# A two-layer attention and retention trunk on one core: column parts in the first T stages, merged row transposes and y stores, and five smaller moves

## The chip, the cores and the metric

The kernel runs on one core of a Trainium2 chip. A core has five engines, each with its own instruction stream: TensorE (PE, matrix products, with a separate record for loading weights, PEld), VectorE (DVE), ScalarE (ACT), GpSimd (POOL) and SyncE (SP), which issues the DMA transfers here. The metric is the device time of one execution in microseconds (us), as the median of several runs. TensorE's clock is regulated: the profile states the granted clock as a share of full speed.

## The reference

Two layers, 2048 tokens, width 1024. Each layer normalizes x, projects it to 4096 columns (eight parts of 512: queries, keys, values and gate of attention; the same of retention), runs two mixers and adds the product of their gated outputs with w_out.

```python
def hybrid_layer(x, norm_gain, w_in, w_out, rel_bias, cos, sin):
    hn = rms_norm(x, norm_gain)
    aq, ak, av, ag, rq, rk, rv, rg = jnp.split(hn @ w_in, cuts, axis=-1)
    ya = chunked_rel_attention(aq, ak, av, rel_bias)      # 8 heads of 64
    yr = chunkwise_retention(rq, rk, rv, cos, sin)        # 4 heads of 128
    y = jnp.concatenate([ya * silu(ag), yr * silu(rg)], axis=-1)
    return x + y @ w_out
```

Attention works on chunks of 64 tokens, each over its own chunk and the eight before, with a learned bias per clipped distance, and a softmax. Retention rotates q and k by position (the tables cos and sin), multiplies within a chunk by a decay, carries a 128x128 state per head from chunk to chunk, and normalizes each head's output by its root mean square. After two layers there is a last normalization. All inputs and outputs are f32.

## The kernel before

**Precision.** Products are made of halves in f16: a value is a high half and a low half (the rest), and a product is three matmuls (high x high, high x low, low x high). So nearly every tensor stands twice: hTh and hTl are the two halves of the normalized tokens, transposed (features on the partitions), whT and wlT those of the weights, rot the halves of the rotated q and k, pq those of the softmax's exponentials.

**Tiling.** The tokens are cut into four blocks n of 512 (tiles of 128: a = 0 to 3), and the heads into four groups s (two attention heads, hx = 0 and 1, and one retention head). For each layer l, group s and block n there is a T stage, `dense_T` (L609): four sections j = 0 to 3 (attention q, attention k, retention k and q), each of 24 matmuls of 512 columns (L731) into an accumulator of the pool psD, which has two buffers; `evacuate` copies each out of it and makes its halves, on ACT, DVE and by DMAs. Then there is a V stage, `dense_V` (L738): for each tile a of 128 tokens 24 matmuls (L752) give the values and the gates; ACT takes them out (v, gt, rv, L760 to L763), and DVE makes the rests and finishes the gate (L766 to L770). gt has a ring of five buffers. After four groups, `wout` makes the output projection (dO, L1105), adds x, and prepares the next layer's tokens; `wout_first` does the beginning of it for the first tokens already in the last group: it loads y from DRAM, squares and scales it, splits it in halves (rhy and rly) and has them transposed (L236, L237).

**Attention and retention of a block** run between the matmuls of the next block's stages, as a generator of 24 steps, one unit (a, hx) every three. For a unit, `qk` makes the logits S on TensorE (L800, L801); DVE adds the bias and takes the maximum in one instruction (L804), and multiplies it and adds a constant (L806); ACT takes the exponential (L807) and its high half (L809), POOL the rest (L810); a DMA on SP transposes both (pT, L812). Two units later `pv` multiplies with the values (L820 to L822), and `out_` divides by the sum, multiplies by the gate into ya, and stores it (L826, L827, L832, L835). `retention` does likewise for its head: products r (L860), state sh and its rest (L864, L868), the norm (a DVE instruction L920, a power on POOL L921), and yr, which is stored by itself (L925, L927).

**What sets the order.** The order is written out by hand: `run` takes steps from a dense stage and steps the attention beside it, and at each step (a tick) `later(k, ...)` work that is due is issued; `push` enters side work (weights, token rows, tables), of which `pull` takes pieces. In the first group the rows of tokens 4 to 15 are normalized, split and transposed while the stages already run. Each engine does its instructions in order; the order on SP is set by a scheduler. A tile's buffer is reused in turn by tag: "sc" and "pq" (two each) hold the logits and the halves of a unit, and at the layer end also the rows of y; "tabc", "tabs", "qq" and "swp" (one each) hold the rotary tables and what is swapped, and in wout the transposed y.

Of the kernel before, what the change touches and what calls it, by code (L numbers as in the profile page):

```python
# [18 lines left out]
P = 128  # L19
# [8 lines left out]
def hybrid_trunk(ctx: ExitStack, tc: tile.TileContext, x, pos, gain, gcol, w_in, w_out, rel, fgain,  # L28
# [33 lines left out]
    pool.memset(mhalf, -0.5)  # L62
    invf_sb = cp.tile([P, 1], F32, tag="invf", name="invf_sb")
# [6 lines left out]
    tab_d = [dp.tile([2, P, 512], F32, tag=f"tab{n}", name=f"tab{n}") for n in range(NS)]  # L70
# [12 lines left out]
    def tables(n, wk):  # L83

        ang, k, r, k2 = wk
# [40 lines left out]
        for hf in range(2):  # L126
            sl = slice(hf * 64, hf * 64 + 64)
            cs = slice(hf * 256, hf * 256 + 256)
            sp.dma_start(tab_d[n][0, 0:64, cs], k2[sl, :])
            sp.dma_start(tab_d[n][0, 64:128, cs], k2[sl, :])  # L130
            sp.dma_start(tab_d[n][1, 0:64, cs], ang[sl, :])
            sp.dma_start(tab_d[n][1, 64:128, cs], r[sl, :])
# [82 lines left out]
    def hT_of(l, n):  # L215
        if (l, n) not in hT:
            hT[l, n] = (hp.tile([P, KT, 512], F16, tag="hTh", name=f"hTh{l}_{n}"),
                        hp.tile([P, KT, 512], F16, tag="hTl", name=f"hTl{l}_{n}"))
        return hT[l, n]

    def row_pair(nm):
        return (b2.tile([P, 1280], F16, tag="sc", name=f"rh{nm}")[:, 0:D],
                b2.tile([P, 1280], F16, tag="pq", name=f"rl{nm}")[:, 0:D])
# [11 lines left out]
    def transpose_rows(rows, dh, dl):  # L235
        sp.dma_start_transpose(out=dh, in_=rows[0])  # L236
        sp.dma_start_transpose(out=dl, in_=rows[1])  # L237

    class Tok:


        def __init__(self, t, xt, rows):
            self.t, self.x, self.rows, self.nm = t, xt, rows, f"n0_{t}"
            self.hh, self.hl = (h_[:, :, t % 4 * P:(t % 4 + 1) * P] for h_ in hT_of(0, t // 4))
# [21 lines left out]
        def hi(self):  # L266
            if self.rows:
                self.rw = (self.rows[:, 0:D], self.rows[:, D:2 * D])
                act.activation(self.rw[0], self.x, AF.Copy)
                return  # L270
            for h in range(2):
                act.activation(self.hh[:, h * KT // 2:(h + 1) * KT // 2, :], self.pt[h], AF.Copy)

        def lo(self):
            if self.rows:
                dve.tensor_tensor(self.rw[1], self.x, self.rw[0], op=ALU.subtract)
                return
# [4 lines left out]
        def dma(self):  # L282
            transpose_rows(self.rw, self.hh, self.hl)
# [324 lines left out]
    def dense_T(l, s, n, g, st):  # L608
        hh, hl = hT[l, n]  # L609
        nm = f"{l}_{s}_{n}"  # L610
        st.tabc = b1.tile([P, 512], F32, tag="tabc", name=f"tabc{nm}")
        st.tabs = b1.tile([P, 512], F32, tag="tabs", name=f"tabs{nm}")
        def tab_load():
            while n not in tab_done:
                pull(1)
            sp.dma_start(st.tabc, tab_d[n][0])
            sp.dma_start(st.tabs, tab_d[n][1])
# [9 lines left out]
        def evacuate(j, ps):  # L627
            if j == 0:
                st.q = b2.tile([P, 2, 2, 512], F16, tag="q", name=f"q{nm}")
                qq = b1.tile([P, 2, 512], F16, tag="qq", name=f"qq{nm}")  # L630
# [10 lines left out]
            elif j == 1:  # L641
                st.k = b3.tile([P, 2, 512], F16, tag="k", name=f"k{nm}")
                kk = b1.tile([P, 2, 512], F16, tag="swp", name=f"kk{nm}")
                kh, kl = kk[:, 0, :], kk[:, 1, :]
                act.activation(kh, ps, AF.Copy, scale=2.0 ** -16)

                def k_rest():
                    dve.scalar_tensor_tensor(out=kl, in0=ps, scalar=2.0 ** -16, in1=kh, op0=ALU.mult, op1=ALU.subtract)
                    sp.dma_start(st.k[0:64, 0, :], kh[0:64, :])
                    sp.dma_start(st.k[64:128, 1, :], kh[64:128, :])  # L650
                    sp.dma_start(st.k[64:128, 0, :], kl[0:64, :])
                    sp.dma_start(st.k[0:64, 1, :], kl[64:128, :])

                soon(k_rest)
            else:
                w = 5 - j
                rot = b2.tile([P, w, 512], F16, tag=f"rot{j}", name=f"rot{nm}_{j}")
                if j == 2:
                    raw = rot[:, 1:3].rearrange("p a c -> p (a c)").bitcast(F32)
                else:  # L660
                    raw = b1.tile([P, 512], F32, tag="qq", name=f"raw{nm}")
                act.activation(raw, ps, AF.Copy, scale=2.0 ** -16)

                def swap(rot=rot, raw=raw, j=j):
                    swp = b1.tile([P, 512], F32, tag="swp", name=f"swp{nm}_{j}")
# [20 lines left out]
                    later(d, turned(raw, raw, st.tabc, ALU.mult))  # L686
                    later(d + 1, turned(swp, swp, st.tabs, ALU.mult))
# [30 lines left out]
        for j in range(2 if first else 0, 4):  # L718
# [19 lines left out]
    def dense_V(l, s, n, g, st):  # L738
        hh, hl = hT[l, n]
# [38 lines left out]
    def attention(l, s, n, g, st, prev, nxt):  # L778
# [4 lines left out]
        ya = {}  # L783

        def qk(a, hx):
# [10 lines left out]
            for j0, j1 in zip(cuts, cuts[1:]):  # L796
# [5 lines left out]
            v = b2.tile([P, 640], F32, tag="sc", name=f"sc{u.nm}")[:, 0:w]  # L802
            m = b2.tile([P, 1], F32, tag="mq", name=f"mq{u.nm}")
            dve.tensor_tensor_reduce(out=v, in0=S[:, 0:w], in1=g.bias[hx][:, 640 - w:640], scale=1.0, scalar=-3.0e38,  # L804
                                     op0=ALU.add, op1=ALU.max, accum_out=m)
            dve.tensor_scalar(m, m, g.nc[:, 0:1], LN_PSC, op0=ALU.mult, op1=ALU.add)  # L806
            act.activation(v, v, AF.Exp, bias=m[:, 0:1], scale=g.c[:, 0:1])  # L807
            pq = b2.tile([P, 1280], F16, tag="pq", name=f"pq{u.nm}")
# [6 lines left out]
        def pv(u):  # L815
            t = 4 * n + u.a
            o = psR.tile([P, 512], F32, tag="small", name=f"o{u.nm}")
            for b, (q_, a_) in enumerate(u.kts):
# [3 lines left out]
                pe.matmul(o[:, 0:65], u.p[:, u.nb + b, :], v_[:, 0:65], start=False, stop=(b == u.nb - 1))  # L822

            def out_():
                rl = b2.tile([P, 1], F32, tag="rl", name=f"rl{u.nm}")
                dve.reciprocal(rl, o[:, 64:65])  # L826
                dve.tensor_tensor(rl, rl, g.ka, op=ALU.mult)  # L827
                if u.hx == 0:
                    ya[u.a] = b2.tile([P, P], F32, tag="ya", name=f"ya{u.nm}")
                y = ya[u.a]  # L830
                vs = slice(u.hx * 64, u.hx * 64 + 64)
                dve.scalar_tensor_tensor(out=y[:, vs], in0=o[:, 0:64], scalar=rl[:, 0:1], in1=st.g[u.a][:, vs],  # L832
                                         op0=ALU.mult, op1=ALU.mult)
                if u.hx == 1:
                    sp.dma_start(y_d[t][:, s * P:(s + 1) * P], y)  # L835
# [3 lines left out]
        ret = retention(l, s, n, g, st)  # L839
# [30 lines left out]
    def decayed(l, s, n, g, st, a):  # L870
        nm = f"{l}_{s}_{4 * n + a}"
        cs = slice(a * P, (a + 1) * P)
        r1 = psR.tile([P, 512], F32, tag="small", name=f"r1{nm}")
        products(r1[:, 0:P], [(st.rk[:, i, cs], st.rq[:, j, cs]) for i, j in ((0, 0), (0, 1), (1, 0))])

        def upper():
            st.dT = b1.tile([P, 2, P], F16, tag="dT", name=f"dT{nm}")
            upper_of(st.dT, r1[:, P:2 * P])

        later(1, lambda: dve.tensor_tensor(r1[:, P:2 * P], r1[:, 0:P], g.msk, op=ALU.mult))  # L880
        later(2, upper)
        later(3, lambda: rest_of(st.dT, r1[:, P:2 * P]))

    def retention(l, s, n, g, st):
        for a in range(4):
# [12 lines left out]
            if not last:  # L898
# [16 lines left out]
                later(3, lambda sh=sh, ns=ns: rest_of(sh, ns))  # L915
# [7 lines left out]
            def fin(t=t, a=a, r2=r2, ss=ss, nm=nm):  # L923
                y = b1.tile([P, P], F32, tag="yr", name=f"yr{nm}")
                dve.scalar_tensor_tensor(out=y, in0=r2[:, 0:P], scalar=ss[:, 0:1], in1=st.g[a][:, P:256],  # L925
                                         op0=ALU.mult, op1=ALU.mult)
# [589 lines left out]
```

## Time and profile before

| | before |
|---|---|
| median of 3 runs | 2094.7 us (2092.41 to 2094.73) |
| the profiled execution | 2094.75 us |
| its span, first to last instruction | 2092.8 us |
| mean granted TensorE clock | 0.991 |
| PE busy | 2004.4 us, 14014 matmuls |
| DVE busy | 1343.8 us |
| ACT busy | 1141.3 us |
| POOL busy | 432.9 us |

In the profile's lines a group is: line of the kernel, engine, operation, what it writes <- what it reads with the shapes, how often; then busy time, mean nanoseconds of one, the idle time of the engine ahead of these instructions, and what ended it. In a timeline a line is start, duration, engine and line, operation; a bracket gives the idle time before it and what ended it. SPq lines are DMAs as SP issues them; their transfer lands later. PE's ends are modelled, so starts are the surer numbers.

### The profile page before, as it was taken

The page shows a single profiled execution, that of the slowest core. Times are in us where ns is not written, and L with a number is a line of the kernel's source. Part 1 is how long each engine was busy: PE and PEld are TensorE (multiplying, and loading weights), DVE is VectorE, ACT ScalarE, POOL GpSimd, SP SyncE. Part 2 cuts the span into 40 slices and gives each one's busy share as a digit, 9 for nine tenths or more (in the row PEclk, how much of TensorE's full clock was granted, in tenths as well). Part 3 has the DMA queues.
Part 4 walks back from the last instruction along what each step waited for, and adds up shares of the span by engine and source line. Part 5 has one row for each costly group of instructions (what it writes and reads, how often), then busy time and mean ns, then how long its engine had stood idle before and what let it go on. Part 6 is the DMA issues. An engine that isn't in the chain of part 4 may idle for free.

```text
span 2092.8 us, 39599 instructions
## 1 busy us (share of the span) xinstructions
PE 2004.4 (96%) x14014; PEld 1049.4 (50%) x14014; DVE 1343.8 (64%) x4031; ACT 1141.3 (55%) x2522; POOL 432.9 (21%) x509
## 2 busy tenths in 40 slices
PE   6888999999999999998999999999999999998998
PEld 4344455555555555444444555555555555554443
DVE  7676666666656666576654666666666667656643
ACT  7455665556565654455444546554655565455432
POOL 1022222222122212121000222222222222222100
PEclk9999999999999999999999999999999999999999
DMA  8767674557476764599965556655655776558874
GB/s 247 171 127 162 136 166 114 115 112 159 110 169 133 161 166 99 113 211 260 219 185 113 120 102 142 130 121 106 155 123 118 178 156 162 117 100 183 212 199 123
DMA packets 645702, 313.65 MB, mean 150 GB/s; under 512 B 459232, under 2 KB 602080, under 8 KB 645504
## 3 DMA queue, kind: packets, MB, share of 16 engines
q1 hardware_dynamic: 645504, 311.12, 66.4%
q8 instruction: 110, 1.80, 0.4%
q14 instruction: 88, 0.72, 0.1%
HBM read 123.26 MB, written 41.98 MB: 79 GB/s over the span
## 4 chain that ended last, share of the span: by engine, by line
PE 55%; DMA 7%; DVE 5%; ACT 3%; issue 1%; SPq 1%; POOL 0%; POOLq 0%; DVEq 0%; ACTq 0%
PE dT L731 18%; PE dV L752 15%; PE dO L1105 12%; DMA pT<-pq 2%; PE r L860 2%; PE S L801 2%; PE S L800 2%; PE o L820 1%; PE o L821 1%; PE o L822 1%; DVE sc L804 1%; DMA swp<-rot 1%; DMA yhy<-rhy 1%; ACT sc L807 1%; ACT pq L809 1%
## 5 line engine op out<-in xcount | busy, mean ns | idle before, releaser
L810 POOL TENSOR_TENSOR pq<-sc,pq 128x640 f16<-128x640 f32 (+4 forms) x256 | 323.8, 1265 | 1175.9 <-issue 590.7
L807 ACT ACTIVATE sc<-sc,mq,cT 128x640 f32<-128x640 f32 (+4 forms) x256 | 218.5, 853 | 558.1 <-DVE mq L806 413.7
L752 PE MATMUL dV<-whV,hTh 128*128 128x512 f16 x1024 | 354.5, 382 | 13.0 <-DVE gt L770 12.8
L731 PE MATMUL dT<-hTh,whT 128*128 128x512 f16 x1008 | 349.4, 382 | 14.7 <-DMA hTh<-hTl 9.6
L752 PE MATMUL dV<-wlV,hTh 128*128 128x512 f16 x1024 | 354.1, 381 | 0.0
L752 PE MATMUL dV<-whV,hTl 128*128 128x512 f16 x1024 | 354.0, 381 | 0.0
L731 PE MATMUL dT<-hTl,whT 128*128 128x512 f16 x1008 | 346.6, 379 | 0.0
L731 PE MATMUL dT<-hTh,wlT 128*128 128x512 f16 x1008 | 346.6, 379 | 0.0
L752 PEld LDWEIGHTS <-hTh 128*128 128x128 f16 x2048 | 197.3, 98 | 227.7 <-DVE gt L770 16.4
L731 PEld LDWEIGHTS <-whT 128*128 128x128 f16 x2016 | 192.9, 98 | 221.6 <-issue 24.1
L804 DVE CUSTOM_DVE_ANT_0 sc<-S,bias 128x640 f32<-128x640 f32 (+4 forms) x256 | 188.4, 736 | 78.8 <-PE S L801 61.1
L1105 PE MATMUL dO<-whO,yly 128*128 128x512 f16 x512 | 194.1, 379 | 2.4 <-DMA yly<-rly 2.4
L1105 PE MATMUL dO<-whO,yhy 128*128 128x512 f16 x512 | 194.0, 379 | 1.2 <-DVE gt L770 0.6
L1105 PE MATMUL dO<-wlO,yhy 128*128 128x512 f16 x512 | 194.0, 379 | 0.0
L809 ACT ACTIVATE pq<-sc 128x640 f16<-128x640 f32 (+4 forms) x256 | 171.5, 670 | 10.9 <-DMA pT<-pq 3.0
L1105 PEld LDWEIGHTS <-yhy 128*128 128x128 f16 x1024 | 99.6, 98 | 115.1 <-issue 0.8
L752 PEld LDWEIGHTS <-hTl 128*128 128x128 f16 x1024 | 99.7, 98 | 105.0 <-issue 2.8
L800 PE MATMUL S<-k,q 128*128 128x128 f16 (+3 forms) x592 | 143.1, 268 | 7.9 <-DVE mq L804 7.9
L731 PEld LDWEIGHTS <-wlT 128*128 128x128 f16 x1008 | 97.2, 98 | 101.8 <-issue 1.1
L820 PE MATMUL o<-v,pT 128*128 128x65 f16 x1120 | 129.6, 193 | 10.2 <-DMA pT<-pq 9.7
L801 PE MATMUL S<-k,q 128*128 128x128 f16 (+3 forms) x592 | 130.5, 268 | 0.0
L820 PEld LDWEIGHTS <-pT 128*128 128x128 f16 x1120 | 105.3, 97 | 49.2 <-DMA pT<-pq 21.3
(350 smaller groups left out, 3352.7 us busy)
## 6 DMA issues: line engine op xcount, KB each, us to landing
q<-qq SPq DMA_DIRECT2D x128, 128.0 KB, 2.7
yyy<-y_d SPq DMA_DIRECT2D x32, 512.0 KB, 4.6
stT<-in_w_in_dram SPq DMA_DIRECT2D x27, 512.0 KB, 4.8
stV<-in_w_in_dram SPq DMA_DIRECT2D x26, 512.0 KB, 4.5
k<-kk SPq DMA_DIRECT2D x128, 64.0 KB, 2.0
swp<-rot SPq DMA_DIRECT2D x64, 128.0 KB, 2.5
tabc<-tab SPq DMA_DIRECT2D x32, 256.0 KB, 2.7
tabs<-tab SPq DMA_DIRECT2D x32, 256.0 KB, 2.9
```

Of the source, the lines that this page charges most:

```text
L731: pe.matmul(ps, w_[:, j, kt, :], h_[:, kt, :], start=(m == 0), stop=(m == 23))
L752: pe.matmul(ps, h_[:, kt, a * P:(a + 1) * P], w_[:, kt, :], start=(m == 0), stop=(m == 23))
L800: pe.matmul(o, st.q[:, hx, 0, cs], k_, start=True, stop=False)
L801: pe.matmul(o, st.q[:, hx, 1, cs], k_, start=False, stop=True)
L804: dve.tensor_tensor_reduce(out=v, in0=S[:, 0:w], in1=g.bias[hx][:, 640 - w:640], scale=1.0, scalar=-3.0e38, op0=ALU.add, op1=ALU.max, accu ...
L807: act.activation(v, v, AF.Exp, bias=m[:, 0:1], scale=g.c[:, 0:1])
L809: act.activation(pq[:, 0:w], v, AF.Copy)
L810: pool.tensor_tensor(pq[:, w:2 * w], v, pq[:, 0:w], op=ALU.subtract)
L820: pe.matmul(o[:, 0:65], u.p[:, b, :], v_[:, 0:65], start=(b == 0), stop=False)
L821: pe.matmul(o[:, 0:64], u.p[:, b, :], v_[:, 65:129], start=False, stop=False)
L860: pe.matmul(out_, w_, m_, start=(i == 0), stop=(i + 1 == len(pairs)))
L1105: pe.matmul(ps, h_[:, kt, :], w_[:, kt, :], start=(m == 0), stop=(m == 23))
```

## The change

1. In the T stages of the first group's blocks n = 1, 2, 3, sections 0 and 1 are made in column parts: token tile by token tile, both sections in turn, 24 matmuls of 128 columns each, with both accumulators open at once.
2. A token's (or y's) high and low rows stand side by side in one tile and are turned by one DMA transpose instead of two; hTh and hTl are one tile, as are the transposed halves of y. The logits' tags "sc" and "pq" become one tile, the rotary tables one, which is loaded in one DMA, and the tables are stored in four DMAs instead of eight. qq, kk, raw and swp become tiles of one tag.
3. y is written into the gate's own tile gt, and attention's and retention's halves of a token tile are stored by one DMA, when both are finished.
4. The logits' scale goes into the reduction as its operand (the minimum of the negative logits in place of the maximum); the multiply and add L806 becomes an addition of a constant on POOL.
5. Both heads of a token tile share one accumulator tile; the reciprocal and its factor are taken for both at once.
6. The rest of retention's state is issued four ticks after, not three.
7. wout_first is pushed after prep_O(l, 1) and the weights' preparation, not ahead of it.

```diff
-        ang, k, r, k2 = wk
+        ang, r, k2, k = (wk[:, i * 256:(i + 1) * 256] for i in range(4))
...
-    def transpose_rows(rows, dh, dl):
-        sp.dma_start_transpose(out=dh, in_=rows[0])
-        sp.dma_start_transpose(out=dl, in_=rows[1])
+    def transpose_rows(rows, dst):
+        sp.dma_start_transpose(out=dst, in_=rows[2])
...
+        second = (l, s) == (0, 0) and n > 0
+        if second:
+            ps = [psD.tile([P, 512], F32, tag="dense", name=f"dT{nm}_{j}") for j in range(2)]
+            m = 0
+            for (j, a) in ((j, a) for a in range(4) for j in range(2)):
+                while g.tdone <= j:
+                    pull(1)
+                cs = slice(a * P, (a + 1) * P)
+                for i, (w_, h_) in enumerate((w_, h_) for (w_, h_) in ((g.h, hh), (g.l, hh), (g.h, hl)) for kt in range(KT)):
+                    kt = i % KT
+                    pe.matmul(ps[j][:, cs], w_[:, j, kt, :], h_[:, kt, cs], start=(i == 0), stop=(i == 23))
+                    m += 1
+                    if m % 32 == 0 and m < 192:
+                        yield
+                if a == 3:
+                    evacuate(j, ps[j])
+            yield
-        for j in range(2 if first else 0, 4):
+        for j in range(2 if first or second else 0, 4):
...
+        def finished(a):
+            left[a] -= 1
+            if left[a] == 0:
+                t = 4 * n + a
+                sp.dma_start(y_d[t].rearrange("p (a s c) -> p a s c", a=2, c=P)[:, :, s],
+                             st.g[a].rearrange("p (a c) -> p a c", a=2))
...
-            v = b2.tile([P, 640], F32, tag="sc", name=f"sc{u.nm}")[:, 0:w]
+            spq = b2.tile([P, 2560], F16, tag="spq", name=f"spq{u.nm}")
+            v, pq = spq[:, 0:1280].bitcast(F32)[:, 0:w], spq[:, 1280:2560]
-            dve.tensor_tensor_reduce(out=v, in0=S[:, 0:w], in1=g.bias[hx][:, 640 - w:640], scale=1.0, scalar=-3.0e38,
-                                     op0=ALU.add, op1=ALU.max, accum_out=m)
-            dve.tensor_scalar(m, m, g.nc[:, 0:1], LN_PSC, op0=ALU.mult, op1=ALU.add)
-            act.activation(v, v, AF.Exp, bias=m[:, 0:1], scale=g.c[:, 0:1])
+            dve.tensor_tensor_reduce(out=v, in0=S[:, 0:w], in1=g.bias[hx][:, 640 - w:640], scale=g.nc[:, 0:1],
+                                     scalar=3.0e38, op0=ALU.add, op1=ALU.min, accum_out=m)
+            pool.tensor_tensor(m, m, lnp, op=ALU.add)
+            act.activation(v, v, AF.Exp, bias=m[:, 0:1], scale=-1.0)
...
+                rl = b2.tile([P, 2], F32, tag="rl", name=f"rl{u.nm}")
+                dve.reciprocal(rl, o2[:, 0:2, 64])
+                dve.tensor_scalar(rl, rl, g.ka[:, 0:1], None, op0=ALU.mult)
+                for hx in range(2):
+                    y = st.g[u.a][:, hx * 64:hx * 64 + 64]
+                    dve.scalar_tensor_tensor(out=y, in0=o2[:, hx, 0:64], scalar=rl[:, hx:hx + 1], in1=y, op0=ALU.mult,
+                                             op1=ALU.mult)
+                finished(u.a)
...
-                later(3, lambda sh=sh, ns=ns: rest_of(sh, ns))
+                later(4, lambda sh=sh, ns=ns: rest_of(sh, ns))
...
-                if n == NS - 1 and s == NSW - 1:
-                    us = []
-                    push(wout_first(l, go, us), 10)
...
                         push(prep_O(l, 1, gO[1], go), 9)
+                        us = []
+                        push(wout_first(l, go, us), 10)
```

More of the change, by code (lines that the diff above doesn't have):

```diff
@@ L62, in hybrid_trunk @@
     pool.memset(mhalf, -0.5)
+    lnp = cp.tile([P, 1], F32, tag="lnp", name="lnp")
+    pool.memset(lnp, LN_PSC)
     invf_sb = cp.tile([P, 1], F32, tag="invf", name="invf_sb")
@@ L69, in hybrid_trunk @@
     x_d = [dp.tile([P, D], F32, tag=f"x_d{t}", name=f"x_d{t}") for t in range(NT)]
-    tab_d = [dp.tile([2, P, 512], F32, tag=f"tab{n}", name=f"tab{n}") for n in range(NS)]
+    tab_d = [dp.tile([P, 2, 512], F32, tag=f"tab{n}", name=f"tab{n}") for n in range(NS)]
     TWO_PI = 6.283185307179586
@@ L125, in tables @@
         yield
[L126 to L132, printed above, removed]
+        parts = wk[:, 0:768].rearrange("p (a c) -> p a c", c=256)
+        for h in range(2):
+            for hf in range(2):
+                sp.dma_start(tab_d[n][h * 64:h * 64 + 64, :, hf * 256:hf * 256 + 256],
+                             parts[hf * 64:hf * 64 + 64, h:3:2 - h])
         tab_done.add(n)
@@ L815, in pv @@
         def pv(u):
-            t = 4 * n + u.a
-            o = psR.tile([P, 512], F32, tag="small", name=f"o{u.nm}")
+            if u.hx == 0:
+                ring["o"] = psR.tile([P, 4, P], F32, tag="small", name=f"o{u.nm}")
+            o2 = ring["o"]
+            o = o2[:, u.hx]
             for b, (q_, a_) in enumerate(u.kts):
@@ L999, in mul @@
         def mul():
-            u.x = xt if on_pe or rows else psS.tile([P, D], F32, tag="S", name=f"xn{nm}")
+            u.x = xt if on_pe or rows is not None else psS.tile([P, D], F32, tag="S", name=f"xn{nm}")
             dve.scalar_tensor_tensor(out=u.x, in0=xt, scalar=u.rs[:, 0:1], in1=gains[l].b, op0=ALU.mult, op1=ALU.mult)
@@ L1273, in hybrid_trunk @@
     sp.dma_start(invf_sb, invf)
-    t0 = tables(0, [gp.tile([P, 256], F32, tag="gt", name=f"wk{i}") for i in range(4)])
+    t0 = tables(0, b2.tile([P, 2560], F16, tag="spq", name="wk").bitcast(F32)[:, 0:1024])
     go_on(t0)
```

126 lines of the change are left out of this document (60 added, 66 removed).

## The prediction

> **What bounds the kernel now.** I read the page's busy times first, then the stretches of 50 us, then TensorE's waits. The first two lines are of the page, the others of the view by stretches (busy time of PE, PEld, DVE, ACT, POOL, then granted clock, DMA share, GB/s).
>
> ```profile
> span 2092.8 us, 39599 instructions
> PE 2004.4 (96%) x14014; PEld 1049.4 (50%) x14014; DVE 1343.8 (64%) x4031; ACT 1141.3 (55%) x2522; POOL 432.9 (21%) x509
> ...
> 50.00:100.00 50.00, 40.16 (x199) 18.42 (x197) 32.59 (x81) 24.55 (x50) 4.32 (x11) 0.90 0.72 164
> 400.00:450.00 50.00, 50.00 (x395) 27.45 (x394) 31.83 (x88) 23.99 (x58) 13.93 (x13) 1.00 0.47 98
> 850.00:900.00 50.00, 43.77 (x310) 22.73 (x309) 30.81 (x89) 28.13 (x58) 10.12 (x10) 0.93 0.70 142
> ```
>
> TensorE is busy 2004.4 of 2092.8 us, and from 400 to 450 for all of it. Work taken from another engine is worth nothing there; only the 88 us in which TensorE is idle, and the places at a clock below 1.00, can be won. They lie in the first head group (before 250 us), at the two layer ends and in the first output projection. TensorE's waits name them (in total, times, longest).
>
> ```profile
> PE dV L752 <- DVE gt L770: 12.8, 6, 4.9
> PE o L820 <- DMA pT<-pq: 9.7, 11, 2.2
> PE dT L731 <- DMA hTh<-hTl: 9.6, 1, 9.6
> PE S L800 <- DVE mq L804: 7.9, 4, 3.3
> PE dT L731 <- DMA hTh<-rhn: 2.8, 1, 2.8
> PE dO L1105 <- DMA yly<-rly: 2.4, 2, 1.7
> PE dT L731 <- issue: 2.2, 1, 2.2
> ```
>
> The profiled execution took 2094.75 us (1.95 around its span); the median of the three runs is 2094.7, so sums made against it stand for the median too.
>
> **Part 1, column parts in the T stages of n = 1, 2, 3 of the first group.** The rows are of the timeline: start, duration, engine, line; in brackets the idle time before.
>
> ```profile
> 64.16 1.22 DVE L276 TENSOR_TENSOR hTl<-hTl,hTl 128x1024 f16<-128x1024 f32 x1
> ...
> 73.10 1.53 SPq L236 DMA_TRANSPOSE hTh<-hTl  x1
> 74.73 2.92 SPq L237 DMA_TRANSPOSE hTl<-hTl  x1
> ...
> 78.91 3.26 PE L731 MATMUL dT<-hTh,whT 128*128 128x512 f16 x8 [9.64 <-DMA hTh<-hTl]
> 82.11 1.89 PE L731 MATMUL dT<-hTh,wlT 128*128 128x512 f16 x8
> 83.84 0.38 PE L731 MATMUL dT<-hTl,whT 128*128 128x512 f16 x1
> ...
> 140.13 1.89 PE L731 MATMUL dT<-hTh,whT 128*128 128x512 f16 x8 [2.21 <-issue]
> ...
> 204.90 1.44 PE L731 MATMUL dT<-hTh,whT 128*128 128x512 f16 x3 [2.81 <-DMA hTh<-rhn]
> ```
>
> At n = 1, TensorE waits 9.64 us for the last token's transposes; its rows were ready at 65.4 (64.16 + 1.22), but SP issued them at 73.10 and 74.73. In parts, the three earlier tokens' columns of both sections are 2 x 3 groups of 24 matmuls of 128 columns. One of 512 columns costs (83.84 - 82.11)/8 = 0.216 us, so a quarter is 0.054 and 24 are 1.3: 6 x 1.3 = 7.8 us of work stand ahead of that token. SP's own queue ahead gets shorter (one transpose for two, four table stores for eight). I take 8.0 of the 9.64 as won, and the first eight at half speed (3.26 against 1.89) as won too, 1.4: -9.4. Bounds: -11.0 (all) and -5.0 (an earlier token still late). The parts cost some fixed time: 0.002 us more per quarter is 0.36 per stage, +1.1 for three; bounds 0 and 2.
>
> The first two rows here are of the timeline, the last of the DMA view (issues, KB, median us to landing). Both accumulators (psD, two) are now taken at once. Section 1's first part, 1.3 us into the stage, needs the buffer of dense_V's fourth tile, where it used to be needed 5.2 us in. And that tile's gate (gt, ring of five) now waits for the store of the block before, since y is written into gt itself.
>
> ```profile
> 140.01 0.47 ACT L761 ACTIVATE gt<-dV,ughV 128x256 f32<-128x256 f32 x1
> ...
> 141.24 0.45 SPq L835 DMA_DIRECT2D y_d<-ya  x1
> ...
> y_d<-ya SPq DMA_DIRECT2D x128, 64.0 KB, 2.1
> ```
>
> At n = 2 the stage would start where the idle time began, 137.9, use up the first part by 139.2, and then wait for gt: the store issued at 141.24 lands 2.1 later (the row's median), 143.3, and gt and DVE's rests follow in about 1 us: a stall of about 5 against 2.21 today. SP is less loaded, so I take +2.5 there and, alike, at n = 3: +5.0; bounds 0 and +10. Section 2 then needs section 0's accumulator, whose rest on DVE is queued a tick later: a rest of 512 columns is like the 0.82 of a 640-column reduction (row 877.29 below), +0.7 each, +2.1; bounds 0 and 4.5. The V-stage waits (12.8, the longest 4.9) stay: they end on ACT, where a table is loaded for the gate between other work, and that order is not changed.
>
> ```profile
> 126.54 1.28 ACT L761 ACT_TABLE_LOAD   x1
> ...
> 128.60 0.29 DVE L766 SCALAR_TENSOR_TENSOR v<-dV,v 128x128 f16<-128x128 f32 x1 [3.42 <-ACT rv L762]
> ```
>
> **Part 2, the layer ends.** wout_first, which loads and scales y of the first token, is pushed behind prep_O(l,1). The rows are of the timeline, the last two of the view by stretches (the clock is the third number from the end).
>
> ```profile
> 877.29 0.82 DVE L804 CUSTOM_DVE_ANT_0 sc<-S,bias 128x640 f32<-128x640 f32 x1 [5.11 <-DMA yhy<-rhy]
> ...
> 878.17 0.27 PE L800 MATMUL S<-k,q 128*128 128x128 f16 x1 [3.28 <-DVE mq L804]
> ...
> 1891.00 0.27 PE L800 MATMUL S<-k,q 128*128 128x128 f16 x1 [3.18 <-DVE mq L804]
> ...
> 876.00:884.00 8.00, 5.83 (x18) 2.45 (x18) 3.94 (x13) 5.02 (x9) 1.40 (x1) 0.57 0.44 87
> 1889.00:1897.00 8.00, 5.72 (x22) 2.45 (x21) 4.09 (x14) 5.03 (x9) 1.40 (x1) 0.79 0.44 86
> ```
>
> The rows of y share a buffer with the logits. DVE's reduction stands 5.11 us until their transpose has landed, TensorE 3.28 behind it, and then runs at a clock that means 0.57 over 876 to 884: 0.43 x 8 = 3.4 us of clock, some of it in the idle time, 2.8 taken. The second end is 3.18 and 0.21 x 8 = 1.7, 1.6 taken. Together 10.9. Moved, the rows are written some six ticks later, beside a later unit; that one's reduction may still wait 1 us each time, and the one merged transpose now waits for both table halves: I take -8.9, bounds -10.9 and +2 (the wait goes over to wout's start).
>
> Beside the row 878.17 the Trainium skill, "TensorE: Matmul & The Clock Gate", section "Part 1: The HAM clock gate", says that an idle window of about 3.4 us halves the clock and that a busy one of that length restores it. The trace agrees that the clock falls, and shows it after waits of 3.28 and 3.18 already, a little below that window. By the page the stall of 5 at n = 2 would halve the clock too, which is an estimate of 1.7 more (half of 3.4) for each; the sum without it stands.
>
> **Part 3, merged row transposes, y tiles, stores.** In the first output projection TensorE waits for pT twice, 1.88 and 2.19, and in dO for y (the row yly<-rly above, 2.4): 6.5 together.
>
> ```profile
> 938.66 0.20 PE L820 MATMUL o<-v,pT 128*128 128x65 f16 x1 [1.88 <-DMA pT<-pq]
> ...
> 953.88 0.20 PE L820 MATMUL o<-v,pT 128*128 128x65 f16 x1 [2.19 <-DMA pT<-pq]
> ```
>
> 128 y stores fewer (0.45 us of issue, row 141.24), 30 y transposes and 22 h transposes fewer (1.4 as at 1409.48 below) take some 130 us off SP, but only here and in the first group is TensorE waiting. I take -3.0; bounds -6.5 and 0.
>
> **Part 4, the softmax chain and the smaller moves.** The first six rows are groups by line (busy us, mean ns | idle before), the last two of the timeline.
>
> ```profile
> L804 DVE CUSTOM_DVE_ANT_0 sc<-S,bias 128x640 f32<-128x640 f32 x192 | 157.3, 819 | 69.1 <-PE S L801 51.6 <-DMA yhy<-rhy 10.1 <-PE msV L323 5.9
> L868 DVE SCALAR_TENSOR_TENSOR sh<-sh,state 128x128 f16<-128x128 f16 x120 | 88.2, 735 | 45.3 <-ACT sh L864 45.2
> L827 DVE TENSOR_TENSOR rl<-rl,kaV 128x1 f32<-128x1 f32 x256 | 59.7, 233 | 8.9
> L806 DVE TENSOR_SCALAR mq<-mq,ncT 128x1 f32<-128x1 f32 x256 | 54.8, 214 | 9.1
> ...
> L921 POOL TENSOR_TENSOR rss<-rss,mhalf 128x1 f32<-128x1 f32 x128 | 72.5, 567 | 139.1 <-DVE rss L920 130.6 <-ACT rv L762 7.2 <-DVE m2T L325 1.3
> L742 POOL MEMSET v<- 128x8 f16 x32 | 4.3, 133 | 0.0
> ...
> 1409.48 1.35 SPq L812 DMA_TRANSPOSE pT<-pq  x1
> ...
> 1415.62 0.19 PE L820 MATMUL o<-v,pT 128*128 128x65 f16 x1
> ```
>
> The reduction takes the scale in itself (no more elements, 819 ns stay); L806 (214) goes and a 128x1 add on POOL comes: between the memset's 133 and the power's 567, nearest the memset in kind, so 0.2 taken. The exponential starts between 0.1 sooner and 0.35 later. Cover: the transpose issued at 1409.48 is down by about 1412.9 (the median of its kind is 3.4), its product starts at 1415.62: 2.7 us. So 0; with the cover gone it would be up to 256 x 0.35 = 90. POOL's queue matters: a power waiting for DVE stands ahead of an add. Both heads divided at once takes 256 small DVE operations (L827 233, a reciprocal) off, and the state's rest a round on gets it (735 mean, against 278 for its like undisturbed) out of POOL's way: DVE is 64% busy and TensorE doesn't wait for it in 400 to 450, so 0. For gt waits in later blocks, whose cover is 5.2 us of section 0, and for late adds I take +1; bounds 0 and 5.
>
> **The sum:** -9.4 + 1.1 + 5.0 + 2.1 - 8.9 - 3.0 + 1.0 = -12.1: 2094.75 - 12.1 = 2082.6, said as 2083.
>
> **Rivals.**
> A, the gate held by the store in every block: 31 blocks, gt of the fourth tile waiting for the merged store of both halves. For it: SP's queue is in order, and the store above went out at 141.24, after gt had run. Against: 5.2 us of cover less 2 for ACT and DVE. It decides where the store lands over 3.2 us after gt could run; 0.7 us beyond that in 31 blocks is +22: about 2105, slower.
> B, the stalls only move: token rows wait for SP's order, and wout starts late by what the reduction had waited. Parts 2 and 3 give nothing, part 1 keeps -1.2: 2093, no change.
> C, the add on POOL comes late behind the power (567): over 2.7 us late at a quarter of 256 units by 0.3 is +19: 2102.
> D, more is won: psD isn't waited for (-7), wout's 6.5 go whole (-3.5), and half of the 9.7 of pT (-5): 2067.
> The Trainium skill, "DMA: Bandwidth & Descriptors", section "Rules for kernel authors", wants many small transfers coalesced, and another row of it calls splitting by partition halves useless: both speak for A's opposite. The median of 2.1 us for 64 KB agrees that little of it is data; no row here shows the merged store.
>
> **How the numbers follow.** Forecast 0.50, D 0.10, B 0.16, A 0.14, C 0.10. No change means within 0.2% (4.2 us), about what a measurement of this kernel can tell. Half of B falls under that, half counts as faster: faster 0.68, same 0.08, slower 0.24. The likeliest case's own range is 2070 to 2092; that for 8 in 10 reaches to D's 2067 with some 3 below it and to C's 2102: 2063 to 2102.
>
> **What would show it.** The gap before T of n = 1 falls below 2 us and its clock is 1.00; in n = 2 and 3 a wait of about 5 ahead of section 1's first part, released by gt's rests; no wait above 1 us with a reduction behind a transpose at the layer ends; the 400 to 450 stretch stays at 50.00. Wrong if T stages or wout show new waits above 3 us, or if the pT waits (9.7 in 11) grow.

## The result, and the profile after

The changed kernel takes 2161.98 us (2160.03 to 2163.09) against 2093.55 for the kernel before: a ratio of 1.0326, 95% interval 1.0308 to 1.0344. It is 68 us slower. The prediction was 2083, in a range of 2063 to 2102; both the sign and the range were wrong. Two of the signs that it had named for this came: T stages with new waits above 3 us, and waits for pT that grew.

The page of the changed kernel, its first lines and the line of the granted clock:

```profile
span 2161.3 us, 39793 instructions
## 1 busy us (share of the span) xinstructions
PE 2020.9 (94%) x14446; PEld 1074.5 (50%) x14446; DVE 1218.4 (56%) x3519; ACT 1117.4 (52%) x2522; POOL 525.1 (24%) x766
...
PEclk9989999999999999999999999999999999998999
```

DVE did what was meant: 1218.4 us in place of 1343.8. TensorE's own busy time grew by 16.5 (432 matmuls more in the column parts, and more at a low clock); the rest of the 68 us is idle time, 140.4 us in place of 88.4. TensorE's waits in the changed kernel (in total, times, longest) name what is new:

```profile
PE r L889 <- DVE sh L897: 26.3, 18, 5.8
PE dT L732 <- DVE gt L791: 22.1, 3, 8.3
PE o L850 <- DMA pT<-spq: 19.7, 20, 1.9
PE dV L773 <- DVE gt L791: 10.5, 6, 2.8
PE S L828 <- ACT fj L205: 7.5, 3, 3.4
PE dT L752 <- DVE gt L791: 6.2, 3, 2.8
```

The wait for the token's transpose (9.6) is gone, and the one behind the reduction fell from 7.9 to 2.6. In their place stand the state's rest (sh, 2.4 before), the accumulators (L732), twice the wait for pT, and in the last output projection one for ACT's squares (fj). Where the time went by stage, from the start of the first matmul of each stage (lengths in us):

| stretch | before | after | difference |
|---|---|---|---|
| start to T of the second group | 264.2 | 277.2 | +13.0 |
| groups 2 to 4 of layer 0, to the last V stage | 595.3 | 611.8 | +16.5 |
| last V stage of layer 0 | 34.3 | 34.3 | 0.0 |
| first output projection | 193.0 | 204.4 | +11.4 |
| layer 1, to the last V stage | 785.7 | 797.0 | +11.3 |
| last V stage of layer 1 | 34.2 | 34.3 | +0.1 |
| second output projection, to the end | 186.2 | 202.3 | +16.1 |

Part of the loss in the output projections is clock and not waiting: TensorE is granted 0.98 and 0.95 of its clock there, against 1.00 and 0.99 before, and is busy 5.2 and 6.8 us longer for the same products.

### The profile page after: what moved, and what is told of

It is laid out like the page before. It is cut to its first block, busy times and chain, and to the rows that moved or that the text cites. A ratio compares the mean times of both kernels' runs of the same rounds, so it can differ in the third digit from the quotient of the medians.

```text
span 2161.3 us, 39793 instructions
## 1 busy us (share of the span) xinstructions
PE 2020.9 (94%) x14446; PEld 1074.5 (50%) x14446; DVE 1218.4 (56%) x3519; ACT 1117.4 (52%) x2522; POOL 525.1 (24%) x766
## 5 line engine op out<-in xcount | busy, mean ns | idle before, releaser
L773 PE MATMUL dV<-whV,hT 128*128 128x512 f16 x2048 | 590.8, 381 | 10.5 <-DVE gt L791 10.5
L752 PE MATMUL dT<-hT,whT 128*128 128x512 f16 x1920 | 549.5, 379 | 8.6 <-DVE gt L791 6.2
L836 ACT ACTIVATE spq<-spq,mq 128x640 f32<-128x640 f32 (+4 forms) x256 | 194.9, 761 | 628.7 <-POOL mq L835 628.7
L773 PEld LDWEIGHTS <-hT 128*128 128x128 f16 x3072 | 291.8, 98 | 328.9 <-DVE gt L791 13.4
L838 POOL TENSOR_TENSOR spq<-spq 128x640 f16<-128x640 f32 (+4 forms) x256 | 322.4, 1260 | 415.2 <-issue 351.9
L773 PE MATMUL dV<-wlV,hT 128*128 128x512 f16 x1024 | 353.0, 380 | 0.0
L752 PE MATMUL dT<-hT,wlT 128*128 128x512 f16 x960 | 331.8, 379 | 0.0
L1135 PE MATMUL dO<-whO,yTy 128*128 128x512 f16 x960 | 295.6, 386 | 7.7 <-DVE hT L1138 4.1
L833 DVE CUSTOM_DVE_ANT_0 spq<-S,bias,ncT 128x640 f32<-128x640 f32 (+4 forms) x256 | 203.3, 794 | 97.2 <-PE S L829 59.1
L1135 PE MATMUL dO<-wlO,yTy 128*128 128x512 f16 x480 | 185.4, 386 | 0.0
L850 PE MATMUL o<-v,pT 128*128 128x65 f16 x1120 | 130.3, 194 | 19.9 <-DMA pT<-spq 19.7
```

The source lines that it names most:

```text
L752: pe.matmul(ps, w_[:, j, kt, :], h_[:, kt, :], start=(m == 0), stop=(m == 23))
L773: pe.matmul(ps, h_[:, kt, a * P:(a + 1) * P], w_[:, kt, :], start=(m == 0), stop=(m == 23))
L836: act.activation(v, v, AF.Exp, bias=m[:, 0:1], scale=-1.0)
L838: pool.tensor_tensor(pq[:, w:2 * w], v, pq[:, 0:w], op=ALU.subtract)
L850: pe.matmul(o[:, 0:65], u.p[:, b, :], v_[:, 0:65], start=(b == 0), stop=False)
L1135: pe.matmul(ps, h_[:, kt, :], w_[:, kt, :], start=(m == 0), stop=(m == 23))
```

## The experiments

Each kernel was timed beside the kernel before, whose median lay between 2093.55 and 2097.61 us. So "less" and "more" below are differences of the ratios, times 2093.55; from the changed kernel's 1.0326 they are known to some 5 us.

### One part undone at a time, from the changed kernel

**The shared tile.** The logits v (f32) and the halves pq of a unit get a tile each again, with two buffers each; a pair of rows that lies in them is transposed by two DMAs. The work space of the first tables, which lay in a shared tile, moves to a buffer of q. So this run undoes a little more than the sharing; the main lines of its edit:

```diff
-            spq = b2.tile([P, 2560], F16, tag="spq", name=f"spq{u.nm}")
-            v, pq = spq[:, 0:1280].bitcast(F32)[:, 0:w], spq[:, 1280:2560]
+            v = b2.tile([P, 640], F32, tag="sc", name=f"sc{u.nm}")[:, 0:w]
+            pq = b2.tile([P, 1280], F16, tag="pq", name=f"pq{u.nm}")
```

> The changed kernel with the shared buffer of a unit undone: the logits and the halves have two tiles with two buffers each again, and a pair of rows that lies in them is transposed by two transfers. Theory S (the shared tile makes DVE's reduction wait for the landing of the transpose of two units before, 34.5 us of DVE idle in the changed profile, and this reaches TensorE at the layer ends and in both output projections, where the changed kernel lost 11.5 and 16.1 us): 25 to 35 us less than the changed kernel's 2162, about 2132. Theory H (the state's rest one tick later is what stops TensorE, 26.3 us in 18 waits): no more than 6 less, 2156 to 2162, the waits for sh stay. Theory G (the gate that waits for its store): the same, 2156 to 2162.

Measured: 2134.25, ratio 1.0178 (1.0161 to 1.0195); 31 us less than the changed kernel. Theory S held. In the changed kernel DVE's waits showed the cause (first line), and in the output projection the timeline showed how it reached TensorE: the reduction waits 2.48 us for the transpose of an earlier unit, the exponential and its copy follow on ACT, the squares (fj, into the logits' only PSUM buffer) queue behind them, and the next logits wait for those.

```profile
DVE spq L833 <- DMA pT<-spq: 34.5, 19, 3.4
```

```profile
1983.47 0.88 DVE L833 CUSTOM_DVE_ANT_0 spq<-S,bias,ncT 128x640 f32<-128x640 f32 x1 [2.48 <-DMA pT<-spq]
...
1985.52 0.74 ACT L837 ACTIVATE spq<-spq 128x640 f16<-128x640 f32 x1
1986.16 1.01 ACT L205 ACTIVATE fj<-hT 128x1024 f32<-128x1024 f32 x1
...
1987.34 0.48 PE L828 MATMUL S<-k,q 128*128 128x384 f16 x1 [3.36 <-ACT fj L205]
```

With two tiles, that wait of DVE is no more in the list, and the output projections take 193.6 and 188.8 us again. The profiled executions differ by 28.7 us: 24.3 less in the two output projections, 7.0 less in the two last V stages, 2.6 more elsewhere. The gain lies where DVE's waits were.

The shared tile also undid the gain at the layer ends. There the square of a y row is written into a pair of rows, which is now a whole shared buffer, so it waits for the transpose of the unit before. These are rows of the changed kernel around the end of layer 0:

```profile
917.69 3.50 SPq L238 DMA_TRANSPOSE yTy<-rwy  x1
...
919.00 1.06 ACT L986 ACTIVATE rwy<-yyy 128x1024 f16<-128x1024 f32 x1 [3.52 <-DMA pT<-spq]
...
920.97 0.29 DVE L787 SCALAR_TENSOR_TENSOR v<-dV,v 128x128 f16<-128x128 f32 x1 [4.21 <-ACT rv L783]
...
922.46 0.28 DVE L897 SCALAR_TENSOR_TENSOR sh<-sh,state 128x128 f16<-128x128 f16 x1
...
922.80 0.26 PE L889 MATMUL r<-sh,rot 128*128 128x128 f16 x1 [5.80 <-DVE sh L897]
```

ACT stands 3.52 us in front of its queue, the gate and the values of the V tile come after it, DVE waits 4.21 for those, and the state's rest stands behind them in DVE's queue. TensorE's 3.28 us from before have become 5.80. With two tiles the last V stages fall from 34.3 to 30.5 and 31.1.

**The state's rest**, three ticks after instead of four.

> The changed kernel with the state's rest issued three ticks after, as before. Theory H (that tick is what makes the products of the state wait): the 26.3 us of waits for sh fall to about 3, time about 2140. Theory S (sh is late because DVE's queue is held at the shared tile and by ACT): the waits shrink by less than 8 us in all, 2154 to 2162; the two of 5.7 us at the layer ends turn into waits for something else.

Measured: 2162.14, ratio 1.0312 (1.0293 to 1.0331): not to be told from the changed kernel. Theory H fell. The wait for sh was the last of a row of waits; without it nearly the same time is waited for the transposed y (5.9 us at each layer end, where sh had 5.8 and 5.7) and the gate:

```profile
PE dO L1135 <- DMA yTy<-rwy: 16.1, 5, 5.9
PE dV L773 <- DVE gt L791: 15.2, 12, 4.9
```

**A sixth gate buffer.**

```diff
-            gt = gp.tile([P, 256], F32, tag="gt", name=f"gt{nm}_{a}")
+            gt = gp.tile([P, 256], F32, tag="gt", name=f"gt{nm}_{a}", bufs=6)
```

> The changed kernel with a sixth gate buffer, so that the gate of a tile waits for the store of five tiles before and not four. Theory G (the gate waits for the merged store and holds both accumulators): the waits of the T stages for the gate at n = 2 and 3 of the first group (6.77 and 8.28 us) go, and those at the T starts later (1.3, 2.1, 2.8) too: about 18 less, 2144. If the first accumulator is late for another reason (at n = 1, where no store had been made, the wait was 7.04), at most 6 less: 2156 to 2162.

Measured: 2143.20, ratio 1.0219 (1.0204 to 1.0234): 22 less. Theory G held for the time; the two waits that it named shrank to 3.2 and 4.5 us and did not go. The rows of the changed kernel: at n = 2 and 3 the gate's activation waits for the store on ACT (the rows of n = 2 are shown), and TensorE for the accumulator behind it. At n = 1 (the first row) no store had been made yet, and the wait has another cause (below).

```profile
77.24 1.03 PE L732 MATMUL dT<-hT,whT 128*128 128x128 f16 x8 [7.04 <-DVE gt L791]
...
135.96 2.42 SPq L687 DMA_TRANSPOSE kt<-rot  x1
138.42 0.59 SPq L810 DMA_DIRECT2D y_d<-gt  x1
...
141.06 0.47 ACT L782 ACTIVATE gt<-dV,ughV 128x256 f32<-128x256 f32 x1 [3.47 <-DMA y_d<-gt]
...
142.75 0.50 PE L732 MATMUL dT<-hT,whT 128*128 128x128 f16 x3 [6.77 <-DVE gt L791]
...
216.86 0.39 PE L732 MATMUL dT<-hT,whT 128*128 128x128 f16 x2 [8.28 <-DVE gt L791]
```

ACT's waits for stores in the changed kernel, and what is left of the waits for accumulators with the sixth buffer:

```profile
ACT gt L782 <- DMA y_d<-gt: 36.1, 22, 4.4
```

```profile
PE dT L732 <- DVE gt L791: 13.0, 3, 5.3
```

ACT's line is no longer in the list of the kernel with six. What of the accumulators' wait stays (5.3 at n = 1) has other causes (below).

**Whole columns** in the first group's T stages.

```diff
-        second = (l, s) == (0, 0) and n > 0
+        second = False
```

> The changed kernel with the T stages of the first group's blocks 1 to 3 in whole columns, as before. Theory G: the waits for both accumulators (22.1 us in three) go, and the wait for the last token's transpose comes back at n = 1 only (at most 9.6, less as SP's queue is shorter): 2145 to 2152. If the parts were worth what the prediction said (-9.4 + 8): 2162 to 2166.

Measured: 2157.48, ratio 1.0289 (1.0273 to 1.0304): 8 less, between the two. The 22.1 us of waits go, but others come back: 5.5 at n = 1, 3.2 at n = 2 and 4.7 at n = 3.

**The constant added on DVE** and not on POOL.

```diff
-            pool.tensor_tensor(m, m, lnp, op=ALU.add)
+            dve.tensor_scalar(m, m, LN_PSC, None, op0=ALU.add)
```

> The changed kernel with one edit: the constant is added on DVE and not on POOL. If the step over POOL costs its 18 us beside the other losses too: 2162 - 18 = 2144. If the shared tile's wait hides it there: 2158 to 2162.

Measured: 2146.82, ratio 1.0241 (1.0220 to 1.0262): 18 less. So the addition costs its time in the changed kernel too; pT's waits fall from 19.7 to 9.0. The group and the two rows show why (POOL's duration is minimum/median/maximum in ns):

```profile
L835 POOL TENSOR_TENSOR mq<-mq,lnp x256: 190/192/1170, 79.1 to 2027.2; 128x1 f32<-128x1 f32 x128
```

```profile
299.66 0.19 POOL L835 TENSOR_TENSOR mq<-mq,lnp 128x1 f32<-128x1 f32 x1 [2.99 <-DVE m2V L329]
...
308.72 1.17 POOL L835 TENSOR_TENSOR mq<-mq,lnp 128x1 f32<-128x1 f32 x1 [1.27 <-DVE mq L833]
...
308.56 1.28 DVE L337 SCALAR_TENSOR_TENSOR wlV<-stV,sV,whV 128x1024 f16<-128x1024 f32 x1
```

Alone, it takes 0.19 us, as was forecast. Beside a DVE instruction with two tensors from SBUF, which had started 0.16 us before, it takes 1.17: it ends when the DVE instruction ends. 73 of the 256 additions took over 0.5 us. This is no single case: all 77 that took over 0.3 us overlap a DVE instruction with two tensors from SBUF and end 0.05 us after it, while none of the 70 that started beside a DVE instruction with one tensor from SBUF and one from PSUM (dT, L897) took over 0.19. The same addition on DVE takes 152 to 155 ns, always. The Trainium skill, "GPSIMD Engine Reference", section "1. Specifications", says that GpSimd shares its SBUF interfaces with VectorE and contends with DVE instructions of two SBUF inputs; the trace agrees, with 1.17 against 0.19.

### Together

**Two tiles and a sixth gate buffer.**

> Both undone together: separate tiles for the logits and the halves, and a sixth gate buffer. If the shared tile (28 us by itself) and the gate's store (19 us by itself) are two separate losses, they add: 2162 - 47 = 2115. If they are one chain (a late transposed unit makes the store late), less: 2120 to 2130.

Measured: 2109.91, ratio 1.0085 (1.0069 to 1.0101): 50 less than the changed kernel, where the two alone give 31 and 22. Within the error they add: they are separate losses.

**With the state's rest three ticks after, too.**

> The two before, and the state's rest three ticks after. With the shared tile in place that tick moved nothing, since the wait went over to others. Theory H' (without the shared tile it is a loss of its own: 18.2 us of waits for sh in 15 places): about 15 less than with the two alone, 2100. If the rest is late for other reasons: within 3 us of the two alone.

Measured: 2105.54, ratio 1.0061 (1.0044 to 1.0078): 5 less, with intervals that overlap. So it is not 15, and may be nothing. Of the 17.4 us of waits for sh 2.3 are left; 6.5 of the rest came back at the gates (V stages 10.8 to 15.2, T stages 10.6 to 12.7), and some at y's transposes.

**With whole columns, on top of the three.**

> The three before, and whole columns in the first group's T stages. Theory P (the column parts, freed from the store, are worth what was forecast, some 8 at n = 1 less 5 in the three stages): 0 to 5 more than the three alone. If holding both accumulators costs more than the last token's wait: up to 8 less.

Measured: 2095.21, ratio 1.0009 (1.0000 to 1.0019): 11 less, though no gate waits for a store any more. Theory P fell.

**With the scale by a second DVE instruction, on top of the three**, and **with the scale in the reduction but the constant added on DVE**.

> Separate tiles, a sixth gate buffer, the state's rest three ticks after, and the logits' scale by a second instruction of DVE again (maximum, then L806's multiply and add), in place of the operand in the reduction (878 ns against 819) and the addition on POOL (360 ns in the mean). Theory C (the pT waits, 15.5 us against 9.7 before, come from this longer way to the exponential): 5 to 8 less than the three alone. If the cover of 2.7 us holds: within 3 us of them.

> Separate tiles, a sixth gate buffer, the state's rest three ticks after; the scale stays in the reduction, but the constant is added on DVE (128x1, some 0.2 us) and not on POOL. If the step over POOL costs the 11 us: about 2094. If the reduction's longer time does (878 against 819 ns, 256 times): about 2105.

Measured: 2094.09 (1.0001, 0.9991 to 1.0010) and 2087.14 (0.9966, 0.9955 to 0.9977): 13 and 20 less. It is the step over POOL that costs, and not the reduction's 59 ns more. The scale as the reduction's operand is even a gain, since the exponential no longer takes its scale from a tensor. Groups of the kernel before, then of the one with the addition on DVE:

```profile
L804 DVE CUSTOM_DVE_ANT_0 sc<-S,bias 128x640 f32<-128x640 f32 x192 | 157.3, 819 | 69.1 <-PE S L801 51.6 <-DMA yhy<-rhy 10.1 <-PE msV L323 5.9
...
L807 ACT ACTIVATE sc<-sc,mq,cT 128x640 f32<-128x640 f32 x192 | 176.7, 920 | 430.5 <-DVE mq L806 317.2 <-DVE rl L826 69.7 <-DVE ymy L961 22.7
```

```profile
L838 DVE CUSTOM_DVE_ANT_0 sc<-S,bias,ncT 128x640 f32<-128x640 f32 x192 | 168.5, 878 | 67.2 <-PE S L834 59.4 <-PE msV L332 5.3 <-DMA yTy<-rhy 2.4
L840 DVE TENSOR_SCALAR mq<-mq 128x1 f32<-128x1 f32 x256 | 39.3, 154 | 8.9
L841 ACT ACTIVATE sc<-sc,mq 128x640 f32<-128x640 f32 x192 | 159.0, 828 | 427.9 <-DVE mq L840 325.4 <-DVE rl L863 69.7 <-DVE m2V L334 15.5
```

Reduction +59, the small instruction 154 in place of 214, the exponential 828 in place of 920: 93 ns less from logits to exponentials, without POOL. The Trainium skill, "ScalarE: Activation LUTs", section "What ACT_TABLE_LOAD costs", gives about 93 ns for each such operand of an activation; the trace agrees with 92.

### The column parts by themselves

**The kernel before with the column parts alone.**

> The kernel before with the column parts alone: its gates don't wait for stores, its SP queue is as long as it was. Theory P (parts hide the last token's wait, both accumulators cost little when no store is awaited): 4 to 8 less than before, 2086 to 2090. Theory Q (the fourth tile's accumulator comes free too late whatever the gate waits for): 3 to 12 more than before, 2097 to 2106.

Measured: 2099.49, ratio 1.0027 (1.0017 to 1.0037), 6 more. Theory Q held: the parts lose by themselves. At n = 1 the stage starts 9.8 us earlier, and then waits 10.0 for the fourth V tile's accumulator; that is the longest of:

```profile
PE dT L728 <- DVE gt L787: 15.8, 3, 10.0
```

No store is awaited there. The run's own rows show what holds it: ACT has the gate and the values out by 70.2, but the rests stand on DVE behind a rotation that waits 7.08 us for a swap, whose first half SP issued at 70.94.

```profile
70.94 0.50 SPq L666 DMA_DIRECT2D swp<-raw  x1
...
77.08 0.69 DVE L670 TENSOR_TENSOR raw<-raw,tabc 128x512 f32<-128x512 f32 x1 [7.08 <-DMA swp<-raw]
...
80.07 0.41 DVE L787 SCALAR_TENSOR_TENSOR gt<-gt,dV 128x256 f32<-128x256 f32 x1
```

In the changed kernel the same rotation waits 4.92 us. And the wait was already there in the kernel before, beside the one for the last token's transposes:

```profile
78.11 0.69 DVE L670 TENSOR_TENSOR raw<-raw,tabc 128x512 f32<-128x512 f32 x1 [7.20 <-DMA swp<-raw]
...
81.10 0.41 DVE L770 SCALAR_TENSOR_TENSOR gt<-gt,dV 128x256 f32<-128x256 f32 x1
```

There it cost nothing: TensorE began the stage at 78.91, and section 0 needs only one accumulator. With both needed at once, the fourth V tile's accumulator became the next thing to wait for.

**Another order of the parts**: three of section 0, three of section 1, then the fourth of each, so that the second accumulator is needed later.

```diff
-            for (j, a) in ((j, a) for a in range(4) for j in range(2)):
+            for (j, a) in ((0, 0), (0, 1), (0, 2), (1, 0), (1, 1), (1, 2), (0, 3), (1, 3)):
```

> Separate tiles, a sixth gate buffer, the state's rest three ticks after, the constant added on DVE (2087 so far), and the column parts in another order: three parts of section 0, three of section 1, then the fourth of each. So the second accumulator is needed 4.0 us into the stage and not 1.3. If the parts lose because both accumulators are needed at once: each of the three waits falls by up to 2.7, time 2079 to 2082. If the wait is for something else (the last token, section 2): 2086 to 2089.

Measured: 2085.37, ratio 0.9954 (0.9936 to 0.9971), not to be told from the 2087.14 (0.9955 to 0.9977) without it; it lies between the two expectations. The waits for accumulators fell from 12.0 us in three to 2.6 in one, and in the profiled executions the second group began 7.2 us sooner; but the spans end only 2.7 us apart (2087.4 and 2084.7). The other 4.5 us are lost in groups 2 to 4 (2.3) and layer 1 (2.2), which this edit does not touch; why is not settled.

### What is left that gains

**Two tiles, six gate buffers, the rest three ticks after, L806 on DVE; whole columns everywhere, or parts at n = 1 alone.**

> Separate tiles, a sixth gate buffer, the state's rest three ticks after, the logits' scale on DVE as before, and whole columns in the first group: five parts of the change undone, what is left is the merged transposes and stores, both heads divided at once and the later push of wout_first. If the two gains of the last runs (10 for whole columns, 11 for the scale on DVE) add: 2105 - 21 = 2084, ten below the kernel before. If they are the same ten (both ease DVE in the first group): 2092 to 2096.

> As the last, with column parts in block n = 1 alone, where the last token comes late. If the parts cost only where both accumulators are awaited (n = 2 and 3): 3 to 8 less than whole columns everywhere, about 2079. If the wait for both accumulators costs as much at n = 1: the same within 3.

Measured: 2085.26 (0.9956, 0.9943 to 0.9968) and 2078.55 (0.9922, 0.9908 to 0.9937). The gains add (22 less than the three alone, where 11 and 13 were found one at a time), and at n = 1 the parts are worth 7. At n = 2 and 3 they cost some 16: with the same other edits and parts in all three blocks the ratio was 1.0001.

**The latter with the scale in the reduction and the constant added on DVE**, and **with the other order of parts**.

> The same five, but with column parts in block n = 1 only, in the order of the change. From 2079 with the scale by L806 on DVE; if the addition alone on DVE is worth 7 against it, as between the two runs before, 2072.

> The last one with the other order of parts in n = 1. If holding both accumulators is what waits there (7.2 us): 2.7 less than with the order of the change; if not, the same within 2.

Measured: 2076.69 (0.9915, 0.9900 to 0.9930) and 2076.52 (0.9907, 0.9891 to 0.9923); neither is to be told from 2078.55, so the 7 expected from the addition on DVE did not show here, nor the 2.7 from the order. They beat both kernels: 18 us under the kernel before. The page of the first of them:

```profile
span 2075.0 us, 39068 instructions
## 1 busy us (share of the span) xinstructions
PE 2005.5 (97%) x14158; PEld 1058.9 (51%) x14158; DVE 1313.5 (63%) x3775; ACT 1118.4 (54%) x2522; POOL 434.7 (21%) x510
```

DVE is busy for 95 us more here than in the changed kernel, which is 85 us slower. The earlier push of wout_first was not tried.

## Why the prediction was wrong

Undone one at a time, the parts give, by the difference of their ratio to 1.0326 (times 2093.55): shared tile 31, gate's store 22, addition on POOL 18, column parts 8, state's rest nothing that can be told. That is 79 in all; undone together, with the parts kept at n = 1, they give 86 (1.0326 - 0.9915). What is left of the change then gains 18 against the kernel before. (That 86 lost and 18 won make the 68 measured is the same subtraction and proves nothing more.) The parts that are left, the merged transposes and stores and both heads divided at once above all, were not undone one by one.

- **The shared tile: not in the sum at all.** The prediction gave the merge of "sc" and "pq" no term; it spoke of the buffer only at the layer ends, where the rows of y shared it with the logits before, too. Two buffers were split by who frees them: v by POOL's rest, pq by the transpose's landing. In one tile the reduction, first in the chain, waits for what frees the last (34.5 us in 19 waits), and DVE's queue stands with it. This is the largest error, 31 us.
- **The fourth V tile's accumulator: right mechanism, too small.** +5.0 for n = 2 and 3 (bounds 0 and 10) was for stalls of about 5 against 2.2 before; they were 6.77 and 8.28 against 2.2 and 2.8, so 10.0 more and not 5.0. That SP was less loaded did not help at n = 2: y was ready at 136.4, but a transpose (kt) that SP had begun at 135.96 held the store until 138.42. At n = 1 the prediction put -9.4 and no such stall; it was 7.04. The start came 10.2 us earlier, as said, and 7 of it was given back to a wait that the kernel before had hidden: the swap of 7.20 us.
- **The parts' other two terms were right.** Section 2's wait was taken as +2.1 and is 2.2 in two places (PE dT from DVE qk). The fixed time was taken as 0.002 us a quarter; quarters at full clock follow each other every 0.056 us in the median, against 0.054. (192 quarters make 0.38 a stage, not the 0.36 of the prediction.)
- **The gate's wait in all later blocks** was taken as +1 with 0 to 5. The sixth buffer gives 22 in all; in the profiled executions 6.5 of it before the second group, 9 in groups 2 to 4, 3 in layer 1.
- **The addition on POOL: taken at 0.** The duration alone was right (0.192 in the median), the bound (0.35 later) was not: it took the nearest undisturbed rows, though the same fence held one that was disturbed, the state's rest with 735 ns against 278 for its like. The power on POOL, too, took 1667 ns once in the kernel before, against 548 in the median. Taking the addition off POOL gives 18. Rival C had the price (19) but another mechanism, a power ahead of it, so the price is luck. The reduction, taken to stay at 819 ns, takes 878; the exponential's 92 ns less, which stood in no term, outweigh that.
- **The layer ends**: the reduction's wait went, as forecast, and nothing was won, since the wait went over to sh through ACT. With two tiles, the rest three ticks after, the scale on DVE and a sixth gate buffer, the last V stages gain 4.5 and 3.8 in the profiled execution, 8.3 against 8.9 forecast; the output projections then begin with 2.3 us of waiting for the transposed y, which is within these lengths. The mechanism and the size were right, for a kernel that this change was not.
- **Merged transposes and stores**: -3.0 forecast in the first output projection. In the eleven traces with two tiles it takes 191.1 to 195.0 us, against 193.0 before: no gain that can be told, and no run has the merged transposes and stores alone.
- **DVE's smaller load**: taken at 0. No run shows that 125 us less of DVE's time bought anything, and none tests it by itself.
- Rival A was right in what it named, a gate held by its store, but not in its place; it had 0.7 us in each of 31 blocks, while ACT waits for a store in 22 places, for 0.15 to 4.45 us, and TensorE stands behind five of them at the start of a T stage. That its price of +22 is what undoing it gave is luck. B, "the stalls only move", is what the layer ends did. The chances were wrong in that A and C were alternatives: both losses came, and together, and the largest was in no rival.

## What to carry to other kernels

A tile that is merged to save a transfer is freed by the last of its users; ask of each merged pair which user came first before, and who is queued behind the instruction that now waits. A buffer that is written in place holds its ring until the store has landed, so compare the store's landing with the buffer's next turn, or give the ring a buffer more. An instruction put on another engine to spare the first one is priced in a chain by its slowest rows and not by its median. And before a wait is taken away, look for the one that ends beside it: the swap's 7.20 us stood beside the 9.64 of the transpose, in the same trace.

## What the runs showed of the hardware

A 128x1 addition on POOL takes 0.19 us, and up to 1.17 beside a DVE instruction that reads two tensors from SBUF; beside one that reads one from SBUF and one from PSUM it stays at 0.19. An exponential over 640 columns takes 828 ns with a constant scale and 920 with a scale from a tensor; DVE's reduction with a constant scale takes 819, and 878 with one from a tensor.
